# Transposes and products of two recurrent heads issued one step later, three results moved to other PSUM banks

## The chip, the cores and the metric

One Trainium2 chip, one core. The number is device microseconds (us) of one execution. Engines are named as in the profile: PE (TensorE matmul), PEld (TensorE weight load), DVE (VectorE), ACT (ScalarE), POOL (GpSimd), SP (SyncE, which issues nearly all DMAs). PSUM, where PE writes its results, has 8 banks of 2 KB per partition.

## The reference

One layer of a diffusion backbone with three recurrent branches, on 640 tokens (512 latent, 128 context) of width 1024, all in float32:

```
h   = RMSNorm(x) * (1 + scale1) + shift1
z   = h @ W_in                                   # cut into the columns of all branches
A   = HGRN2(q, f_fwd, f_bwd, i, g)               # 4 heads of 128, both directions
B   = RWKV7(...)                                 # 8 heads of 64, both directions
C   = mLSTM(q, k, v, o, gates)                   # 4 heads of 128, both directions
mix = (sig(gA)*(A @ P_A) + sig(gB)*(B @ P_B) + sig(gC)*(C @ P_C)) @ W_out
x   = x + gate1 * RMSNorm(mix)
x   = x + gate2 * RMSNorm(SwiGLU(RMSNorm(x) * (1 + scale2) + shift2))
```

HGRN and mLSTM are chunkwise. HGRN, for each chunk, makes the state S' = exp(b_end) * S + (k * exp(b_end - b))^T v and reads it with q * exp(b). mLSTM does C' = carry * C + (w * k)^T [v, 1], an inner product k^T q under a causal mask with exponential weights D, and num = D [v, 1] + w_inter * (q C). The outputs are the 640 tokens and the final states of the context.

## The kernel before, in words

Everything is kept transposed, features on partitions and the 640 tokens along the free axis. A projection by a 1024 x 128 block of weights is two halves of 320 tokens, each 8 blocks of k times 3 matmuls (`half_proj`): float32 is split into a high and a low part in a reduced format, and hi*hi, hi*lo and lo*hi are added up in one PSUM bank of the pool `pj`. The weights of a projection are two tiles of 512 columns, each split by ACT (`whi`, a cast, L344) and then DVE (`wlo`, the rest, L262), from a ring of 4 tiles (`WSB`), so two projections ahead at most.

The kernel goes through RWKV (up to about 605 us of the profile), then HGRN and mLSTM together (605 to 1003 us, the stage that is changed), then the merge, W_out and the feed-forward part. In the changed stage PSUM is cut into `pj` (4 banks: the halves of projections, and the accumulators `acc` and `col_` of the modulation rows), `ps` with tag "A" (2 banks: the results of mLSTM, among them `btr`, `ms`, `kv`, `kx`, `np_`, `nq`) and `ps2` with tag "H" (2 banks: HGRN's `btr`, `htr`, `hpr`, `hg_`, `hop`).

The order of the work is written as generators. `hgrn_head` and `mlstm_head` yield after each piece; `weave` takes two steps of HGRN for one of mLSTM; and `run_over` adds, after each step, `FILL2[head]` of a step of `fill`: the projections of the merge gates (evacuated by ACT at L572 into `gs`, which has two buffers and is written to DRAM) and the modulation's matmuls. What comes earlier in that order has precedence, but it is not the order on the engines. A list scheduler works through the program before it is compiled, with costs of its own for each instruction, takes on each engine the earliest instruction that it believes ready, and lets a tile wait for the release of its buffer or bank. The result is one fixed queue per engine, run in order: an instruction that waits holds up everything behind it on its engine, and the scheduler's costs are not the chip's.

A head of HGRN: project `hi` into `hT1`, transpose it to `v` by token (`by_token`, 5 transposes into 2 banks and 2 ACT copies), project `hq`, the two `hf`; exponentials and scans; for each direction transpose the keys `kh` (L1136), copy to `hkt` (ACT, L1138), multiply with `v` to `hpr` and add to the states (DVE, L268); then seven `level`s of intra-chunk products with POOL, DVE and ACT work; `hop`, output. A head of mLSTM: project `mv`, `mq`, `mk` and transpose two of them by token; `ms` = k^T q, masked on DVE to `mS`; for each direction the weights D, the state products `kv` and `kx`, then `np_` = D [v, 1] (copied by ACT to `nd`, L1394) and `nq` = q C (added by DVE, L268).

In the groups below, `hT` stands for HGRN's `hT1` and `hT2`, `nd` for the two `nd0`, `nd1`, and L277 is the line of all matmuls, L262 and L268 those of all DVE helper operations.

Of the kernel before, what the change touches and what calls it, by code (L numbers as in the profile page):

```python
# [8 lines left out]
F32 = mybir.dt.float32  # L9
# [33 lines left out]
RB2 = 2  # L43
HTB = 3
ORDER = "hoahoahoahoa" + "gga" * 12
FILL2 = (0.13, 0.14, 0.11, 0.16)
WSB = 4
RAWB = 3
YBB = 2
# [206 lines left out]
def build(tc, **A):  # L256
# [36 lines left out]
    with ExitStack() as top:  # L293
# [8 lines left out]
        pj_p = [pj_pool(6)]  # L302
# [742 lines left out]
        with ExitStack() as ms, ExitStack() as mr:  # L1045
# [33 lines left out]
            def hgrn_head(hd):  # L1079
                t1 = ht.tile([128, T], F32, name="hT1")  # L1080
                yield from mixproj(f"hi{hd}", h, to_sb(t1))
                v = hb.tile([128, 5, 128], F32, name="hv")
                by_token(v, t1, ps2, "H")
                yield
                q = hb.tile([128, T], F32, name="hq")
                yield from mixproj(f"hq{hd}", h, to_sb(q, 128.0 ** -0.5))
                yield
                b, kd, qe, SSs, zs, ls, khs, ebs = [], [], [], [], [], [], [], []
                D2 = range(2)
# [39 lines left out]
                for d in D2:  # L1129

                    S = hb.tile([128, 4, 128], F32, name=f"hS{d}")
                    sp.dma_start(S[:, 0 if d == 0 else 3], A["shg"][:, d * 4 + hd])
                    cs = (0, 1, 2, 4) if d == 0 else (3, 2, 1, 4)
                    tr = ps2.tile([128, 4, 128], F32, name="htr", tag="H")
                    for i, c in enumerate(cs):
                        pe.transpose(tr[:, i], khs[d][:, c * 128:(c + 1) * 128], ident)  # L1136
                    kt = ht.tile([128, 4, 128], F32, name="hkt", bufs=1)
                    act.copy(kt, tr)  # L1138
                    pr = ps2.tile([128, 4, 128], F32, name="hpr", tag="H")
                    for i, c in enumerate(cs):  # L1140
                        mm(pr[:, i], kt[:, i], v[:, c])
                    for i, c in enumerate(cs[:3]):
                        cn = c + 1 if d == 0 else c - 1
                        stt(S[:, cn], S[:, c], ebs[d][:, c:c + 1], pr[:, i], ALU.mult, ALU.add)
                    fs = ht.tile([128, 128], F32, name="hfs")
                    act.copy(fs, pr[:, 3])
                    sp.dma_start(A["ohg"][:, d * 4 + hd], fs)
                    SSs.append(S)
                    yield
# [192 lines left out]
            def mlstm_head(hd, mt):  # L1342
                k = mt.tile([128, T], F32, name="mk", bufs=1)
                yield from whole(mixproj(f"mv{hd}", h, to_sb(k)))
                by_token(v1, k, ps)
                q = mt.tile([128, T], F32, name="mq", bufs=1)
                k = mt.tile([128, T], F32, name="mk", bufs=1)
                yield from whole(mixproj(f"mq{hd}", h, to_sb(q)))
                yield from whole(mixproj(f"mk{hd}", h, to_sb(k, 128.0 ** -0.5)))
                kt = mt.tile([128, 5, 128], F32, name="mkt", bufs=1)  # L1350
                by_token(kt, k, ps)
                Sd = [mt.tile([128, 5, 128], F32, name=f"mS{d}", bufs=1) for d in range(2)]
                for c0, n in CP:
                    s_ = ps.tile([128, 4, 128], F32, name="ms", tag="A")
                    for i in range(n):
                        sl = slice((c0 + i) * 128, (c0 + i + 1) * 128)
                        mm(s_[:, i], k[:, sl], q[:, sl])
                    for d in range(2):
                        mul(Sd[d][:, c0:c0 + n], s_[:, :n], caus[:, d].unsqueeze(1).to_broadcast([128, n, 128]))
                nds, rds = [], []  # L1360
                for d in range(2):
                    ub = mt.tile([128, T], F32, name="ub", bufs=1)
                    sp.dma_start(ub, ud[d * 4 + hd:d * 4 + hd + 1].to_broadcast([128, T]))
                    D = mt.tile([128, 5, 128], F32, name="mD", bufs=1)
                    for c in range(5):
                        ts(D[:, c], c5(ub)[:, c], tcol("a", d, hd, c), 0.0, ALU.add, ALU.min)
                    act.activation(D, D, AF.Exp)
                    mul(D, D, Sd[d])
                    nd = mt.tile([128, 5, 129], F32, name=f"nd{d}", bufs=1)
                    Cs = mt.tile([128, 4, 129], F32, name="Cs", bufs=1)  # L1370
                    sp.dma_start(Cs[:, 0 if d == 0 else 3], A["scn"][:, d * 4 + hd])
                    vs = mt.tile([128, 5, 129], F32, name="vs", bufs=1)
                    pool.tensor_tensor(vs, v1, tcol("ws", d, hd).unsqueeze(2).to_broadcast([128, 5, 129]), ALU.mult)
                    kv = ps.tile([128, 3, 160], F32, name="kv", tag="A")
                    kx = ps.tile([128, 160], F32, name="kx", tag="A")
                    for i, c in enumerate((0, 1, 2) if d == 0 else (3, 2, 1)):
                        mm(kv[:, i, 0:129], kt[:, c], vs[:, c])
                        stt(Cs[:, c + 1 if d == 0 else c - 1], Cs[:, c], csb[:, d, hd, c:c + 1], kv[:, i, 0:129],
                            ALU.mult, ALU.add)
                    mm(kx[:, 0:129], kt[:, 4], vs[:, 4])  # L1380
                    C2 = mt.tile([128, 129], F32, name="Cn", bufs=1)
                    act.copy(C2, kx[:, 0:129])
                    sp.dma_start(A["ocn"][:, d * 4 + hd], C2)
                    yield
                    for c0, n in CP:
                        np_ = ps.tile([128, 3, 160], F32, name="np_", tag="A")
                        for i in range(n):
                            mm(np_[:, i, 0:129], D[:, c0 + i], v1[:, c0 + i])
                        nq = ps.tile([128, 3, 160], F32, name="nq", tag="A")
                        for i in range(n):  # L1390
                            c = c0 + i
                            if c < 4:
                                mm(nq[:, i, 0:129], q[:, c * 128:(c + 1) * 128], Cs[:, c])
                        act.copy(nd[:, c0:c0 + n], np_[:, :n, 0:129])  # L1394
                        for i in range(n):
                            c = c0 + i
                            if c < 4:
                                stt(nd[:, c], nq[:, i, 0:129], tcol("wi", d, hd, c), nd[:, c], ALU.mult, ALU.add)
                        yield
                    rd = mt.tile([128, 5], F32, name=f"rd{d}")  # L1400
                    den = nd[:, :, 128]
                    stt(rd, den, -1.0, den, ALU.mult, ALU.max)
                    tt(rd, rd, tcol("em", d, hd), ALU.max)
                    dve.reciprocal(rd, rd)
                    nds.append(nd)
                    rds.append(rd)
                hh = mt.tile([128, 5, 128], F32, name="mh", bufs=1)
                ssq = mt.tile([128, 5], F32, name="ssq")
                sq = mt.tile([128, 128], F32, name="msq")
                for c in range(5):  # L1410
                    ts(hh[:, c], nds[0][:, c, 0:128], rds[0][:, c:c + 1])
                    stt(hh[:, c], nds[1][:, c, 0:128], rds[1][:, c:c + 1], hh[:, c], ALU.mult, ALU.add)
                    act.activation(sq, hh[:, c], AF.Square, accum_out=ssq[:, c:c + 1])
                act.activation(ssq, ssq, AF.Sqrt, scale=1.0 / 128, bias=col(COL_EPS6))
                dve.reciprocal(ssq, ssq)
                for c in range(5):
                    ts(hh[:, c], hh[:, c], ssq[:, c:c + 1])
                og = mt.tile([128, T], F32, name="og", bufs=1)

                yield from need(24 + hd)  # L1420
                sp.dma_start(og, gates[24 + hd])
                yield
                ts(og, og, hmn[:, hd:hd + 1], hmn[:, hd:hd + 1])
                for c0, n in ((0, 4), (4, 1)):
                    tr = ps.tile([128, 4, 128], F32, name="mhtr", tag="A")
                    for i in range(n):
                        pe.transpose(tr[:, i], hh[:, c0 + i], ident)
                    mul(c5(yc[:, hd])[:, c0:c0 + n], tr[:, :n], c5(og)[:, c0:c0 + n])
# [403 lines left out]
```

## Time and profile before

| | |
|---|---|
| runs | 1619.7, 1621.25, 1624.62 us; median 1621.25 |
| the profiled execution | 1623.08 us, of which the span of its instructions is 1621.3 us |
| PE busy | 1540.6 us (95% of the span), PEld 1418.1 us |
| DVE busy | 1131.9 us (70%) |
| ACT busy | 782.8 us (48%) |
| POOL busy | 275.7 us (17%) |
| mean granted TensorE clock | 0.976 |

The chain that ended last is given to PE for 23% of the span by name and little else: PE is the engine that the rest is measured against. A row of the timeline is: start in us, duration in us, engine, line, operation, output and inputs, shape, how many instructions were merged in it, and in brackets how long the engine had been idle just before it and what ended that.

### The profile page before, as it was taken

What the parts mean: (1) busy time and instruction counts of PE and PEld (TensorE: products, weight loads), DVE (VectorE), ACT (ScalarE), POOL (GpSimd) and SP (SyncE); (2) the same over time, 40 slices, a digit from 0 to 9 for tenths busy, and PEclk for the clock granted to TensorE, in tenths of its full rate; (3) what the DMA queues carried; (4) which work ended last, traced back from release to release, by engine and by line L of the source; (5) the groups of instructions that cost most, each with busy time, mean ns of one, the idle gap of its engine ahead of it and who ended that gap; (6) DMA issues with size and microseconds to landing.
All of it is one profiled execution on the core that took longest, in us unless ns stands there. A gap on an engine that the chain in (4) does not pass through costs nothing. (4 is left out here: it accounts for less than half of the span.)

```text
span 1621.3 us, 34724 instructions
## 1 busy us (share of the span) xinstructions
PE 1540.6 (95%) x14194; PEld 1418.1 (87%) x14194; DVE 1131.9 (70%) x2355; ACT 782.8 (48%) x1546; POOL 275.7 (17%) x347
## 2 busy tenths in 40 slices
PE   6999999999999988899999999999999999999996
PEld 2988888888877778889798988999999999999996
DVE  6788788687777644786758578772887386586576
ACT  5364455454454334666476666223553343243244
POOL 2110110110110100211303031000123241341211
PEclk9999999999999969999999999999989999999998
DMA  9222222212122313232332332643512222222322
GB/s 361 71 75 88 74 71 80 95 50 88 66 73 95 113 49 103 70 99 78 94 100 85 100 101 95 201 145 108 155 37 86 95 79 76 82 88 68 99 94 97
DMA packets 63791, 157.35 MB, mean 97 GB/s; under 512 B 7432, under 2 KB 27912, under 8 KB 63504
## 3 DMA queue, kind: packets, MB, share of 16 engines
q1 hardware_dynamic: 63488, 155.13, 29.5%
q8 instruction: 111, 1.82, 0.5%
q14 instruction: 48, 0.39, 0.1%
q10 hardware_dynamic: 144, 0.00, 0.0%
HBM read 136.73 MB, written 18.37 MB: 96 GB/s over the span
## 5 line engine op out<-in xcount | busy, mean ns | idle before, releaser
L277 PE MATMUL pj<-h_hi,whi 128*128 128x320 f32 x1560 | 495.0, 320 | 5.4 <-ACT t L396 2.7
L277 PE MATMUL pj<-h_lo,whi 128*128 128x320 f32 x1560 | 494.4, 317 | 0.0
L277 PE MATMUL pj<-h_hi,wlo 128*128 128x320 f32 x1560 | 493.2, 317 | 0.0
L262 DVE TENSOR_TENSOR wlo<-raw,whi 128x512 fp32r<-128x512 f32 (+1 forms) x318 | 228.5, 726 | 130.7 <-ACT whi L344 106.2
L277 PEld LDWEIGHTS pj<-h_hi,whi 128*128 128x128 f32 x1560 | 296.3, 191 | 12.0 <-ACT t L396 3.7
L277 PEld LDWEIGHTS pj<-h_lo,whi 128*128 128x128 f32 x1560 | 296.7, 190 | 3.2
L277 PEld LDWEIGHTS pj<-h_hi,wlo 128*128 128x128 f32 x1560 | 296.9, 190 | 2.8
L344 ACT CAST whi<-raw 128x512 fp32r<-128x512 f32 (+1 forms) x264 | 156.8, 599 | 219.6 <-PE pj L277 209.4
L277 PE MATMUL pj<-a,whi 128*128 128x320 f32 x704 | 155.3, 309 | 0.0
L277 PEld LDWEIGHTS pj<-a,whi 128*128 128x128 f32 x704 | 117.7, 188 | 0.2
L277 PE MATMUL pj<-a,wlo 128*128 128x320 f32 x352 | 108.8, 309 | 0.0
L277 PE MATMUL pj<-t_hi,whi 128*128 128x320 f32 x288 | 89.1, 309 | 1.1 <-DVE u L262 1.1
L277 PE MATMUL pj<-t_hi,wlo 128*128 128x320 f32 x288 | 89.1, 309 | 0.1
L277 PE MATMUL pj<-t_lo,whi 128*128 128x320 f32 x288 | 89.0, 309 | 0.0
L262 DVE TENSOR_TENSOR wlo<-sm,whi 128x512 fp32r<-128x512 f32 x72 | 68.1, 946 | 11.4 <-ACT whi L1684 8.5
L1684 ACT CAST whi<-sm 128x512 fp32r<-128x512 f32 x72 | 44.4, 621 | 64.4 <-PE pj L277 50.2
L1678 POOL TENSOR_TENSOR sm<-raw 128x512 f32<-128x512 f32 x36 | 49.0, 1360 | 110.3 <-DMA raw<-wff 72.5
L277 PEld LDWEIGHTS pj<-a,wlo 128*128 128x128 f32 x352 | 66.1, 188 | 0.0
L277 PE MATMUL pj<-hl,whi 128*128 128x320 f32 x256 | 56.5, 310 | 0.6 <-ACT hl L1462 0.6
L1684 ACT CAST whi<-raw 128x512 fp32r<-128x512 f32 x54 | 33.5, 620 | 45.6 <-PE pj L277 37.7
L277 PEld LDWEIGHTS pj<-t_hi,whi 128*128 128x128 f32 x288 | 54.1, 188 | 1.3 <-DVE u L262 1.3
L277 PE MATMUL acc<-raw,sc 128*32 128x256 f32 (+1 forms) x320 | 40.7, 437 | 14.8 <-DMA raw<-wada 14.8
(659 smaller groups left out, 2988.0 us busy)
## 6 DMA issues: line engine op xcount, KB each, us to landing
raw<-wmix SPq DMA_DIRECT2D x76, 512.0 KB, 3.5
raw<-wada SPq DMA_DIRECT2D x48, 512.0 KB, 5.6
raw<-wff SPq DMA_DIRECT2D x44, 512.0 KB, 3.7
gates<-gs SPq DMA_DIRECT2D x64, 160.0 KB, 1.8
raw<-wff SPq DMA_DIRECT2D x24, 384.0 KB, 3.2
gs<-gates SPq DMA_DIRECT2D x24, 320.0 KB, 3.1
raw<-wbr SPq DMA_DIRECT2D x12, 512.0 KB, 4.3
raw<-wout SPq DMA_DIRECT2D x8, 512.0 KB, 5.0
```

What stands on the lines that cost most here:

```text
L262: dve.tensor_tensor(out, a, b, op)
L277: newest[0] = pe.matmul(out, lhsT=lhsT, rhs=rhs, start=start, stop=stop, skip_group_check=more).ins
L344: act.copy(hi[:, :w], raw[:, o:o + w])
L1678: pool.tensor_tensor(o, x, y, op)
L1684: act.copy(hi, x)
```

## The change

Three pieces of work are placed elsewhere in the generators, three tiles come from another PSUM pool, and the rates at which `fill` is mixed in are lowered by 0.01.

- HGRN: `by_token` of `v` comes after the projection `hq` and no longer before it (the number of yields stays).
- HGRN: a yield stands between the copy `hkt` and the products `hpr` (two more per head).
- mLSTM: a yield stands between the transposes of k and the products `ms` (one more per head). The woven stage has 171 steps, where it had 159.
- mLSTM: `ms`, `kx` and `nq` take a bank of `pj` (4 banks) and no longer one of `ps` "A" (2 banks).

```
--- before.py
+++ after.py
@@ -43,7 +43,7 @@
 RB2 = 2
 HTB = 3
 ORDER = "hoahoahoahoa" + "gga" * 12
-FILL2 = (0.13, 0.14, 0.11, 0.16)
+FILL2 = (0.12, 0.13, 0.1, 0.15)
 WSB = 4
 RAWB = 3
 YBB = 2
@@ -1079,11 +1079,11 @@
             def hgrn_head(hd):
                 t1 = ht.tile([128, T], F32, name="hT1")
                 yield from mixproj(f"hi{hd}", h, to_sb(t1))
+                yield
                 v = hb.tile([128, 5, 128], F32, name="hv")
-                by_token(v, t1, ps2, "H")
-                yield
                 q = hb.tile([128, T], F32, name="hq")
                 yield from mixproj(f"hq{hd}", h, to_sb(q, 128.0 ** -0.5))
+                by_token(v, t1, ps2, "H")
                 yield
                 b, kd, qe, SSs, zs, ls, khs, ebs = [], [], [], [], [], [], [], []
                 D2 = range(2)
@@ -1136,6 +1136,7 @@
                         pe.transpose(tr[:, i], khs[d][:, c * 128:(c + 1) * 128], ident)
                     kt = ht.tile([128, 4, 128], F32, name="hkt", bufs=1)
                     act.copy(kt, tr)
+                    yield
                     pr = ps2.tile([128, 4, 128], F32, name="hpr", tag="H")
                     for i, c in enumerate(cs):
                         mm(pr[:, i], kt[:, i], v[:, c])
@@ -1349,9 +1350,10 @@
                 yield from whole(mixproj(f"mk{hd}", h, to_sb(k, 128.0 ** -0.5)))
                 kt = mt.tile([128, 5, 128], F32, name="mkt", bufs=1)
                 by_token(kt, k, ps)
+                yield
                 Sd = [mt.tile([128, 5, 128], F32, name=f"mS{d}", bufs=1) for d in range(2)]
                 for c0, n in CP:
-                    s_ = ps.tile([128, 4, 128], F32, name="ms", tag="A")
+                    s_ = pj_p[0].tile([128, 4, 128], F32, name="ms", tag="pj")
                     for i in range(n):
                         sl = slice((c0 + i) * 128, (c0 + i + 1) * 128)
                         mm(s_[:, i], k[:, sl], q[:, sl])
@@ -1372,7 +1374,7 @@
                     vs = mt.tile([128, 5, 129], F32, name="vs", bufs=1)
                     pool.tensor_tensor(vs, v1, tcol("ws", d, hd).unsqueeze(2).to_broadcast([128, 5, 129]), ALU.mult)
                     kv = ps.tile([128, 3, 160], F32, name="kv", tag="A")
-                    kx = ps.tile([128, 160], F32, name="kx", tag="A")
+                    kx = pj_p[0].tile([128, 160], F32, name="kx", tag="pj")
                     for i, c in enumerate((0, 1, 2) if d == 0 else (3, 2, 1)):
                         mm(kv[:, i, 0:129], kt[:, c], vs[:, c])
                         stt(Cs[:, c + 1 if d == 0 else c - 1], Cs[:, c], csb[:, d, hd, c:c + 1], kv[:, i, 0:129],
@@ -1386,7 +1388,7 @@
                         np_ = ps.tile([128, 3, 160], F32, name="np_", tag="A")
                         for i in range(n):
                             mm(np_[:, i, 0:129], D[:, c0 + i], v1[:, c0 + i])
-                        nq = ps.tile([128, 3, 160], F32, name="nq", tag="A")
+                        nq = pj_p[0].tile([128, 3, 160], F32, name="nq", tag="pj")
                         for i in range(n):
                             c = c0 + i
                             if c < 4:
```

## Rows read from the trace of the kernel before

**Rows 1.** Windows (us; busy of PE, PEld, DVE, ACT, POOL; clock, DMA share, GB/s), changed stage
```profile
605.00:700.00 95.00, 84.65 (x650) 80.74 (x648) 59.68 (x103) 53.16 (x95) 14.96 (x16) 0.93 0.31 98
700.00:792.00 92.00, 87.70 (x884) 82.97 (x884) 65.09 (x147) 59.09 (x119) 17.60 (x20) 1.00 0.28 91
792.00:884.00 92.00, 89.23 (x893) 84.06 (x892) 67.17 (x151) 59.25 (x120) 19.00 (x20) 1.00 0.30 91
884.00:977.00 93.00, 88.80 (x891) 83.90 (x890) 65.93 (x149) 59.28 (x119) 17.60 (x20) 1.00 0.30 90
977.00:1003.00 26.00, 24.34 (x361) 21.50 (x359) 23.28 (x70) 15.52 (x40) 2.80 (x4) 1.00 0.21 65
```

**Rows 2.** Waits of PE, 605 to 1003 us (waiter, releaser: total us, times, longest)
```profile
PE nq L277 <- ACT nd L1394: 5.8, 6, 1.5
PE hpr L277 <- ACT hkt L1138: 5.4, 3, 5.0
PE btr L557 <- ACT hT L396: 4.2, 1, 4.2
PE ms L277 <- ACT mkt L558: 3.5, 3, 1.5
```

**Rows 3.** Timeline of PE, first head, around the two long stalls
```profile
612.36 0.69 PE L557 MATMUL btr<-cst,hT 128*128 128x128 f32 x2 [4.16 <-ACT hT L396]
612.70 0.61 PE L277 MATMUL pj<-h_hi,whi 128*128 128x320 f32 x1
...
617.68 0.31 PE L277 MATMUL pj<-h_lo,whi 128*128 128x320 f32 x1
617.83 0.30 PE L277 MATMUL pj<-h_hi,wlo 128*128 128x320 f32 x1
...
669.45 0.31 PE L277 MATMUL pj<-h_hi,wlo 128*128 128x320 f32 x1
674.73 2.07 PE L277 MATMUL hpr<-hv,hkt 128*128 128x128 f32 x8 [4.96 <-ACT hkt L1138]
...
679.00 0.33 PE L277 MATMUL pj<-h_hi,whi 128*128 128x320 f32 x1
```

**Rows 4.** Windows of 10 us around these two stalls
```profile
610.00:620.00 10.00, 7.64 (x37) 7.60 (x38) 9.69 (x20) 7.28 (x13) 0.00 (x0) 0.66 0.06 15
670.00:680.00 10.00, 5.28 (x24) 5.28 (x25) 7.53 (x15) 4.21 (x9) 0.81 (x1) 0.66 0.27 89
```

**Rows 5.** Timeline of ACT, first head
```profile
609.96 1.28 ACT L1308 ACT_TABLE_LOAD   x1 [3.01 <-DVE mrow L1280]
...
672.33 1.54 ACT L1194 ACTIVATE hT<-hT 128x640 f32<-128x640 f32 x2 [1.82 <-DVE hT L262]
```

**Rows 6.** Timeline of DVE, first head, two weight splits
```profile
619.33 1.29 DVE L262 TENSOR_TENSOR wlo<-raw,whi 128x512 fp32r<-128x512 f32 x2
...
673.02 0.68 DVE L262 TENSOR_TENSOR wlo<-raw,whi 128x512 fp32r<-128x512 f32 x1
```

**Rows 7.** Timeline of ACT, second head
```profile
776.58 0.44 ACT L572 ACTIVATE gs<-pj 128x320 f32<-128x320 f32 x1 [2.61 <-DMA gates<-gs]
...
788.50 0.48 ACT L1394 COPY nd<-np__10419 128x387 f32<-128x387 f32 x1
```

**Rows 8.** Timeline of PE, second head
```profile
777.44 1.16 PE L277 MATMUL ms<-mq,mk 128*128 128x128 f32 x8 [1.47 <-ACT mkt L558]
778.83 1.16 PE L277 MATMUL hpr<-hv,hkt 128*128 128x128 f32 x8 [0.23 <-ACT hkt L1138]
...
789.03 0.94 PE L277 MATMUL nq<-Cs,mq 128*128 128x129 f32 x6 [1.26 <-ACT nd L1394]
...
791.66 0.49 PE L277 MATMUL nq<-Cs,mq 128*128 128x129 f32 x2 [0.66 <-ACT nd L1394]
```

**Rows 9.** Timeline of DVE, second head
```profile
788.86 0.35 DVE L268 SCALAR_TENSOR_TENSOR Cs<-Cs,csb,kv 128x129 f32<-128x129 f32 x1
...
796.28 0.34 DVE L268 SCALAR_TENSOR_TENSOR nd<-nq,TM,nd 128x129 f32<-128x129 f32 x1
```

More of the change, by code (lines that the diff above doesn't have):

```diff
@@ L45 @@
 ORDER = "hoahoahoahoa" + "gga" * 12
-FILL2 = (0.13, 0.14, 0.11, 0.16)
+FILL2 = (0.12, 0.13, 0.1, 0.15)
 WSB = 4
@@ L1081, in hgrn_head @@
                 yield from mixproj(f"hi{hd}", h, to_sb(t1))
+                yield
                 v = hb.tile([128, 5, 128], F32, name="hv")
-                by_token(v, t1, ps2, "H")
-                yield
                 q = hb.tile([128, T], F32, name="hq")
                 yield from mixproj(f"hq{hd}", h, to_sb(q, 128.0 ** -0.5))
+                by_token(v, t1, ps2, "H")
                 yield
@@ L1138, in hgrn_head @@
                     act.copy(kt, tr)
+                    yield
                     pr = ps2.tile([128, 4, 128], F32, name="hpr", tag="H")
@@ L1351, in mlstm_head @@
                 by_token(kt, k, ps)
+                yield
                 Sd = [mt.tile([128, 5, 128], F32, name=f"mS{d}", bufs=1) for d in range(2)]
                 for c0, n in CP:
-                    s_ = ps.tile([128, 4, 128], F32, name="ms", tag="A")
+                    s_ = pj_p[0].tile([128, 4, 128], F32, name="ms", tag="pj")
                     for i in range(n):
@@ L1374, in mlstm_head @@
                     kv = ps.tile([128, 3, 160], F32, name="kv", tag="A")
-                    kx = ps.tile([128, 160], F32, name="kx", tag="A")
+                    kx = pj_p[0].tile([128, 160], F32, name="kx", tag="pj")
                     for i, c in enumerate((0, 1, 2) if d == 0 else (3, 2, 1)):
@@ L1388, in mlstm_head @@
                             mm(np_[:, i, 0:129], D[:, c0 + i], v1[:, c0 + i])
-                        nq = ps.tile([128, 3, 160], F32, name="nq", tag="A")
+                        nq = pj_p[0].tile([128, 3, 160], F32, name="nq", tag="pj")
                         for i in range(n):
```

## The prediction

> **What bounds the kernel now.** I read the busy times first (PE 95% of the span), then the windows of the changed stage, then PE's waits in it, and for each wait the timeline of PE and of the engine that ended it. The windows [rows 1] show that PE is idle for 10.35, 4.30, 2.77, 4.20 and 1.66 us of the five stretches, 23.3 us in all; everywhere else PE works through projections. So a stall of PE that goes is worth its length, unless PE meets another wait straight after it, and nothing else in the stage is worth anything. Four waits carry 18.9 of these 23.3 us: `nq` 5.8, `hpr` 5.4, `btr` 4.2, `ms` 3.5 [rows 2]. These are exactly the operations that the change touches, so what can be gained is bounded, and the question is what PE meets next.
>
> Two stalls cost more than their length. After 4.16 and 4.96 us of standing [rows 3] the granted clock of the two windows is 0.66 on average [rows 4], which mixes the two levels, 1.2 and 2.4 GHz. PE comes back at the lower one: from 612.36 to 617.68 and from 674.73 to 679.00, where the timeline shows starts 0.27 us apart and not 0.15, so half of 5.32 and half of 4.27 us is lost, 2.7 and 2.1 us. In the later heads, where no stall is over 1.5 us [rows 2], the clock stays at 1.00 [rows 1].
>
> **The change part by part.** The sum is made against the profiled execution, 1623.08 us (1621.3 of span and 1.8 around it); it lies 1.83 us above the median of the runs, so I take the sum off the median.
>
> No instruction is added or removed: the same transposes, products, copies and DMAs are issued, 12 steps of the woven order hold nothing new, and the lower rates of `fill` over 171 steps instead of 159 put about as many of its steps beside each head (0.13 x 39 = 5.1 and 0.12 x 42 = 5.0 in the first). Counting the yields by hand, the fill projections come to within one or two steps of where they were; one shift matters: the fill projection of the first head that came right after the first `hpr` now comes before it. The cost of these at 0 rests on PE having projections to run in the meantime; without that cover, a step is worth at most the 1.66 us that PE is idle at the stage's end [rows 1].
>
> *Moving `by_token` of v (term A).* In the first head PE stands 4.16 us because the transposes wait for ACT's copy of `hi` [rows 3], and ACT stood 3.01 us for a scan of the mLSTM gates on DVE before a table load [rows 5]. The matmuls of `hq` follow the transposes at once [rows 3], so their weights were there. In the new order PE runs `hq` from 608.2: 48 matmuls, 0.15 us from one start to the next at the full clock (617.68 to 617.83 [rows 3]), are 7.2 us, to 615.4, and the five transposes end by about 616. But the next projection needs a `wlo` that DVE makes only at 619.33 [rows 6], behind the chain of gate operations that keeps it busy 9.69 of 10 us [rows 4], and those are not moved. PE then waits until about 620 instead, some 4 us, and the clock most likely falls again. The bounds are 0 and 4.16 + 2.7 = 6.8 us; I take 0.5. In the later heads there was no such wait (one in all [rows 2]), so nothing is gained there.
>
> *The yield before `hpr` (term B).* The long one of three waits is 4.96 us at 674.73 [rows 3]. The copy `hkt` came late because ACT, in its own order, stood for DVE before the exponentials of a level (1.82 us at 672.33) [rows 5]. With the fill projection ahead of `hpr`, PE goes on with it: the row at 669.45 is the sixth of 12 matmuls on its first weight tile, ended by 669.76; it does 6 more (0.9 us) and then lacks the second tile, whose `wlo` DVE makes from 673.02 to 673.70 [rows 6]. So it stands about 3.0 us, not 4.96: 1.9 us gained. Whether a stall of 3 us still costs clock no row shows, since the nearest are 1.5 us (no) and 4.16 us (yes). I add 0.6 of the 2.1 us: 2.5. Bounds 0 and 7.1. `hpr`, the state sums behind it on DVE and the DMA of the final state come a step later; DVE has other work then, and the levels do not read the states.
>
> The Trainium skill (TensorE: Matmul & The Clock Gate, Part 1) says that the low rate is the default and that activity releases it; by that alone, a stall that still counts as idle keeps the whole loss and B is 1.9, one that does not gives B 4.0. Its Part 4 says that transposes do not count as matmul activity in the same way, which speaks against term A, where ten transposes of the gates would come right after the new stall: the slow stretch with transposes in it was 5.32 us and the one without 4.27 [rows 3], so A would lose half of 1.05, about 0.5 us, and be 0. Neither changes the sum by more than the bounds above.
>
> *The yield before `ms`, and its banks (term C).* `ms` reads only the projections of q and k; it waited for the copies `mkt`, because with two banks in "A" its bank was that of the transposes. In the second head this is 1.47 us at 777.44 [rows 8]. With `pj` it need not wait for that. But ACT itself stood 2.61 us until 776.58 for the DMA that empties `gs` [rows 7], and the second `hpr` waits for a copy behind the same ACT instruction: it came 0.23 us after `ms` [rows 8]. If the queue puts that `hpr` ahead of `ms`, as the new yields make likely, PE stands at the same place for `hkt`, and `ms` no longer covers it. Per head the result lies between -1.4 us (1.16 us of `ms` uncovered and the 0.23) and +1.5; over the three waits 3.5 us is the upper end and -3 the lower. I take 1.0, nearer the middle.
>
> *`nq` and `kx` in `pj` (term D).* `nq` waited for the bank that ACT's copy of `np_` gives back: 1.26 us at 789.03 and 0.66 at 791.66 in the second head [rows 8], with the copy at 788.50 [rows 7]. Its data, the states `Cs` of the first chunks, were there. With its own bank it starts at once, about 787.8, and takes 0.8 us. Then the second `np_` needs a bank of "A", free at 788.98 (the copy) or 789.21 (the last sum out of `kv`) [rows 7, 9], so 0.4 to 0.6 us of waiting comes back. Gained 0.7 to 0.8 of the 1.26 and all of the 0.66, say 1.4 of 1.92. In that ratio the 5.8 us give 4.2; since the queue around it will be another, I take 3.5, bounds 0 and 5.8. `kx` had no wait of its own and counts 0.
>
> *What the moved tiles take from projections (term E).* A bank with `nq` is held until DVE has added it: from 791.66 to 796.62, 5.0 us [rows 8, 9]. The `pj` pool has four banks, a half projection takes 24 x 0.15 = 3.6 us of one and then waits for its evacuation, and `acc` and `gs` hold banks in the same stretch. Bounds: 0 (a bank is always free) and -14 (worked out under the rivals). I take -1.0, nearest to 0, because three of four banks must be out at once.
>
> Sum: 0.5 + 2.5 + 1.0 + 3.5 - 1.0 = 6.5 us off. From 1623.08 that is 1616.6 for a like execution, and from the median 1614.75: I say 1615.
>
> **The rivals.**
> *Given back.* Each stall comes back as a wait one step on: A as a wait for `wlo`, B too with the clock lost again, C as a wait for `hkt`. For it: DVE is all but full where A ends [rows 4], and ACT's late copies have causes that the change leaves alone [rows 5, 7]. Against it: the `nq` waits have no second cause near. A 0, B 0.5, C 0, D 2.0, E -0.5: 2 us, 1619.25.
> *Starved projections.* PE finds no free `pj` bank when a half projection begins, because `ms` and `nq` wait for DVE. Each hold of 5.0 us leaves 1.4 us beyond the 3.6 us of the half that PE can still run. There are five such holds in a head (`ms`, and `nq` twice in each direction), 20 in all; if half of them strike, 14 us is lost against the 7.5 us gained, 6.5 us slower: 1627.75. It decides from the point where three of the four banks are waiting for DVE or ACT. For it: DVE takes 5 us to come to `nq` [rows 8, 9]. Against it: the four banks were never what PE waited for [rows 2].
> *All of it.* The stalls go and PE finds work everywhere: 0.5 + 7.1 + 3.5 + 0.5 (the short `hpr` waits) + 5.8 = 17.4 us, 1604. It needs DVE to make its low parts earlier than now, for which no row speaks.
>
> **How the numbers follow.** Forecast 0.45, given back 0.25, starved 0.20, all of it 0.10. What can be told from no change here is 0.3%, 4.9 us: below 1616.4 or above 1626.1. The forecast's own spread is 1610 to 1619, two thirds of it below 1616.4: 0.30; with all of it 0.10 and a fifth of the second case 0.05, faster is 0.45. Slower is most of the starved case and a trace of the second, 0.17; the rest, 0.38, is no change. The range for 8 in 10 goes from 1607, which leaves out most of the last case, to 1626, which leaves out most of the starved one.
>
> **What would show it.** Right: the waits of PE lose the rows of `nq` on `nd` and `ms` on `mkt`, PE's idle time between 605 us and the stage's end falls from 23 to about 17 us, and the stall at 612 is found some 8 us later, ended by DVE's `wlo`. B is wrong if `hpr` still waits some 5 us for `hkt`, or if the clock stays at 1.00 around 675. C is wrong if `hpr` waits longer for `hkt` in heads two to four than the 0.23 us of now. E shows as waits of a first `pj` matmul for DVE's `nd` or `mS`. The forecast as a whole is wrong if the difference comes from before 605 us or after the stage, where nothing is edited, or if PE's busy time in the stage rises at full clock.

## The result, and the profile after

The changed kernel takes 1676.22 us (median of 4 runs, 1668.16 to 1678.36), the kernel before 1622.16 us (4 runs): a ratio of 1.0335, 95% interval 1.0313 to 1.0358. I had said 1615, with 1607 to 1626 as the range: the sign and the size are both wrong. The profiled execution of after is its fastest, 1668.16 us with a span of 1666.3 us, 45.0 us over the span of before.

First the engines' busy times over the span, from the page of after:

```profile
PE 1545.7 (93%) x14194; PEld 1428.6 (86%) x14194; DVE 1136.4 (68%) x2355; ACT 789.1 (47%) x1548; POOL 276.0 (17%) x347
```

The same 14194 matmuls; PE was busy 1540.6 us before. Then the windows of the changed stage, which now ends about 1048 us and not 1003 (columns as in rows 1):

```profile
605.00:700.00 95.00, 81.04 (x708) 78.18 (x707) 62.00 (x110) 53.77 (x97) 17.16 (x18) 0.94 0.31 99
700.00:803.00 103.00, 90.34 (x849) 86.82 (x849) 66.28 (x146) 59.71 (x119) 18.12 (x20) 0.93 0.26 79
803.00:900.00 97.00, 86.39 (x766) 84.23 (x766) 59.51 (x132) 55.40 (x108) 11.99 (x14) 0.90 0.23 76
900.00:1004.00 104.00, 89.58 (x836) 85.25 (x837) 64.58 (x142) 58.67 (x115) 16.37 (x18) 0.91 0.25 80
1004.00:1048.00 44.00, 34.24 (x467) 30.89 (x468) 33.46 (x95) 23.21 (x55) 9.25 (x11) 0.77 0.24 74
```

The stage is 443 us long and was 398. PE idles 61.4 of them (23.3 in [rows 1]): 38.1 us more. It is busy 381.6 us (374.7 in [rows 1]) though it holds slightly fewer matmuls (3624 in the trace of this stretch, 3671 before: a little of `fill` now comes after it), because the granted clock is 0.77 to 0.94 where it was 1.00 after the first head: 6.9 us more. The two make the 45.0 us; the stretches before and after the stage are as long as they were.

PE's waits in that stage, to be put beside [rows 2]:

```profile
PE hpr L277 <- ACT hkt L1138: 13.2, 4, 3.4
PE mtr L1314 <- ACT PK L1307: 5.8, 1, 5.8
PE kv L277 <- DVE Cs L268: 3.7, 4, 1.1
PE hg__10475 L277 <- DVE hT L262: 2.8, 1, 2.8
...
PE hg__12871 L277 <- DVE rd L268: 2.1, 1, 2.1
...
PE nq L277 <- DVE Cs L268: 1.7, 4, 0.5
```

The waits of `nq` for `nd` and of `ms` for `mkt` are gone, as the change means, and `btr`'s too. In their place stand longer ones: `hpr` in every head, and the levels (`hg_`) of every head, 1.8 to 2.8 us at each of three or four levels, 31 us in all where the levels of before waited 3. No row shows a projection that waits for a bank. PE's timeline of the second head, from the second state product to the last levels, shows why the levels' waits are there:

```profile
787.05 1.16 PE L277 MATMUL hpr<-hv,hkt 128*128 128x128 f32 x8 [3.41 <-ACT hkt L1138]
788.14 1.24 PE L277 MATMUL hg__10297<-hT,hT 128*64 128x64 f32 x20
789.31 2.08 PE L277 MATMUL ms<-mq,mk 128*128 128x128 f32 x8
...
800.21 0.56 PE L277 MATMUL hg__10442<-hT,hT 128*32 128x32 f32 x40 [0.28 <-DVE hT L262]
803.60 0.76 PE L277 MATMUL hg__10475<-hT,hT 128*32 128x32 f32 x40 [2.83 <-DVE hT L262]
806.53 0.76 PE L277 MATMUL hg__10515<-hT,hT 128*32 128x32 f32 x40 [2.17 <-DVE hT L262]
809.11 0.77 PE L277 MATMUL hg__10548<-hT,hT 128*32 128x32 f32 x40 [1.81 <-DVE rd L268]
810.96 0.80 PE L277 MATMUL kv<-vs,mkt 128*128 128x129 f32 x2 [1.08 <-DVE Cs L268]
```

From 781.24 to 820.79 there is not one projection matmul between these rows. In the kernel before, projections filled exactly these gaps; the same levels there, with the first and the last projection matmul of a gap:

```profile
793.33 0.56 PE L277 MATMUL hg__10442<-hT,hT 128*32 128x32 f32 x40
793.82 0.42 PE L277 MATMUL pj<-h_hi,wlo 128*128 128x320 f32 x1
...
795.83 0.31 PE L277 MATMUL pj<-h_hi,whi 128*128 128x320 f32 x1
796.41 0.56 PE L277 MATMUL hg__10475<-hT,hT 128*32 128x32 f32 x40 [0.28 <-DVE hT L262]
...
802.12 0.56 PE L277 MATMUL hg__10548<-hT,hT 128*32 128x32 f32 x40
```

From `hg__10442` to `hg__10548` the levels take 8.8 us before and 8.9 after: they did not get slower, only what ran beside them is gone. Two windows over levels of the second head, first before (a longer one), then after:

```profile
790.00:808.00 18.00, 17.06 (x297) 15.43 (x296) 17.83 (x46) 8.73 (x15) 3.02 (x5) 1.00 0.19 55
```

```profile
799.50:811.00 11.50, 3.32 (x165) 2.67 (x164) 11.41 (x32) 3.81 (x8) 1.96 (x2) 0.61 0.42 125
```

DVE is full in both, 17.83 of 18 and 11.41 of 11.5 us, and the levels wait for it. PE was busy 17.06 of the 18 us beside it and now is 3.32 of the 11.5. The compiled queue of PE says the same. Counted between a head's first `ms` and its `hop`, it holds 78, 83, 78 and 83 projection matmuls in the four heads before, and 0, 0, 0, 0 after. In the second head the tiles are these, in the order of the queue (the numbers rise with the order of the program):

```
before: ... col_  pj_10719 ... hg__10397  nq_10423 ... hg__10442  pj_10719 pj_10745 ... pj_10816 ... nq_10700  hop ...
after:  ... nq_10423 ... hg__10442 hg__10475 hg__10515 hg__10548 ... np__10696  nq_10700  hop  nq_10700  pj_10719 ...
```

`pj_10719` to `pj_10816` are four half projections: the two of the next head's `hi` and two of `fill`'s merge gates, which ACT copies to `hT1` and to `gs`. Later in the program than `nq_10700`, the second direction's `nq`, they ran before it; now the first waits until `nq_10700`, which is of its pool since the change, has its bank. In both queues the first matmuls of all the pool's tiles in this stage stand in the order of their numbers, without an exception.

### The profile page after: what moved, and what is told of

It reads as the page before. It is cut to its first block, busy times and chain, and to the rows that moved or that the text cites. A ratio compares the mean times of both kernels' runs of the same rounds, so it can differ in the third digit from the quotient of the medians.

```text
span 1666.3 us, 34731 instructions
## 1 busy us (share of the span) xinstructions
PE 1545.7 (93%) x14194; PEld 1428.6 (86%) x14194; DVE 1136.4 (68%) x2355; ACT 789.1 (47%) x1548; POOL 276.0 (17%) x347
## 5 line engine op out<-in xcount | busy, mean ns | idle before, releaser
L277 PEld LDWEIGHTS pj<-t_hi,wlo 128*128 128x128 f32 x288 | 54.1, 188 | 0.7 <-DVE wlo L262 0.7
```

What stands on the lines that cost most here:

```text
L277: newest[0] = pe.matmul(out, lhsT=lhsT, rhs=rhs, start=start, stop=stop, skip_group_check=more).ins
```

## The experiments

**Theory (order of the pool):** a pool's banks are given out in the order of the program, so a tile that is ready late, `nq` of the second direction, holds back every projection behind it in the program, and nothing runs beside the levels. **Rivals:** the moved pieces and yields (steps); too few free banks because `ms`, `nq` and `kx` hold them for DVE (count, the prediction's starved case). Each kernel was timed beside the kernel before, whose medians were 1619.9 to 1621.3 us.

### Which part of the change

`steps_only` keeps all moves, yields and rates and takes the three tiles back; `banks_only` is the reverse:

```
 steps_only:  after, with  s_, kx, nq = ps.tile(..., tag="A")
 banks_only:  before, with s_, kx, nq = pj_p[0].tile(..., tag="pj")
```

> The changed kernel with ms, kx and nq back in the two banks of A; the moved pieces, the three yields and the fill rates stay. Theory (order of the pool): the banks of pj are given out in the order of the program, so nq of the second direction, which stands in the program before the projections of the next head, keeps these from starting early, and PE has nothing to run between the levels. Then the moved pieces are harmless: 1612 to 1626 us, and PE idles 20 to 26 us in the stage. Rival (steps): the state products one step later lengthen HGRN's chain, and their waits for hkt (13.2 us in the changed kernel) are the start of the loss: 1645 us or more. Rival (count of banks): as the theory, since no tile is moved.

> The kernel before with only ms, kx and nq moved to pj; no yield, no moved piece, the old fill rates. Order of the pool: nearly the whole loss, 1660 to 1680 us, with no projection matmul on PE between ms and hop of a head. Count of banks: the same time, but with first matmuls of a projection waiting for DVE's nd or mS. Steps: 1630 us or less.

`steps_only` 1627.82 us (ratio 1.0035, 1.0021 to 1.0048), `banks_only` 1686.19 us (1.0388, 1.0369 to 1.0408). The steps cost some 6 us and not 25; the banks cost more alone than with the steps, and a little more than the 1680 us that the theory allowed. In `banks_only` too the queue holds no projection matmul between `ms` and `hop`, and no row shows a projection that waits for `nd` or `mS`, as the count of banks would have it. `steps_only` came out a little over what the theory allowed it: the moves are not harmless, see below.

### Which tile

```
 nq_only:  after, with s_ and kx back in ps "A"
 nq_back:  after, with nq back in ps "A"
```

> The changed kernel with only nq in pj; ms and kx back in A. Order of the pool: the second direction's nq alone stands before the next projections and needs the last states, so the loss stays, 1655 to 1680 us. Count of banks: ms takes two banks and kx one, so without them about half of the loss is left: 1635 to 1650 us. Steps: 1645 us or more here too.

> The changed kernel with nq back in A; ms and kx stay in pj. Order of the pool: ms and kx need only projections, transposes and one POOL product and come early, so the projections of the next head are held back little: 1614 to 1634 us. Count of banks: two banks of ms and one of kx are still taken, so half of the loss is left: 1640 to 1655 us. Steps: 1645 us or more.

`nq_only` 1688.58 us (1.0409, 1.0385 to 1.0433), a little above what was expected; `nq_back` 1631.55 us (1.0052, 1.0036 to 1.0069). It is `nq`.

### Which direction of it, and order or number

```
 nq_d0, nq_d1:  before, with nq = (pj_p[0] if d == 0 else ps)...   or   d == 1
 pj3:           before, with PJ2 = 3
 nq_own:        pj3, with px = tile_pool(bufs=1, space=PSUM);  nq = px.tile(...)
```

> The kernel before with nq in pj for the second direction only. Order of the pool: this nq is the last pj tile before the next head's projections and needs the last of the head's states, so nearly the whole loss of 54 to 67 us is here: 1665 to 1690 us. Count of banks: half of the nq tiles, so at most half of the loss: 1640 to 1655 us.

> The kernel before with nq in pj for the first direction only. Order of the pool: it gets its bank while the first levels still run and the projections can start behind it: 1616 to 1635 us. Count of banks: as many tiles as the second direction's, so the same time as with those, 1640 to 1655 us.

> The kernel before with nq in a PSUM pool of its own of one bank, pj cut from four to three banks. Order of the pool: projections have a bank less, but nothing of mLSTM stands in their pool, so they run ahead again: 1618 to 1640 us, about as the kernel with only pj cut to three. Count of banks: projections have three banks here as they had with an nq that holds one, so the loss stays: 1660 us or more.

> The kernel before with pj cut from four banks to three, one bank unused, nothing else: what a lost bank alone costs. Order of the pool: 1618 to 1635 us. Count of banks: 1650 us or more.

`nq_d1` 1681.79 us (1.0368, 1.0343 to 1.0392): half the tiles, the whole loss. `nq_d0` 1630.86 us (1.0047, 1.0031 to 1.0063). The queue of PE holds 0 projection matmuls beside the levels in each head of `nq_d1`, 68 or 69 in those of `nq_d0`. `nq_own` 1632.90 us (1.0071, 1.0051 to 1.0090), with three banks for projections and `nq` in no one's way: the 60 us are not a matter of number. `pj3` 1642.85 us (1.0131, 1.0112 to 1.0150) is slower than expected, so a bank is worth 21.6 us to the projections: its queue holds 48, 67, 48 and 83 of their matmuls between `ms` and `hop`, and none beside the last three levels of heads one and three. With the same three banks, `nq` out of "A" gains 10 us (1642.85 to 1632.90).

The last pair changes the program order of the same tiles by the weave alone:

```
 hr18_before:  before, with HRATE = 1.8        hr18_d1:  nq_d1, with HRATE = 1.8
```

> nq_d1 (nq of the second direction in pj, nothing else) with the weave at 1.8 steps of HGRN for one of mLSTM and no longer 2: mLSTM's products then stand earlier in the program order against HGRN's levels. Order of the pool: the loss of 60 us against the kernel before depends on that order, and with nq earlier some projections stand behind it beside the levels (25 of them in the first head, 151 in the last, where nq_d1 had none), so this lies at most 25 us above the same weave without the moved tile. Run time holding of banks (count): the moved tile costs 50 to 60 us in this weave too.

> The kernel before with the weave at 1.8: the control for the other run, what the weave costs by itself. No theory fixes it: it shifts the streams against each other; 1625 to 1660 us.

`hr18_before` 1658.08 us (1.0230, 1.0197 to 1.0263), `hr18_d1` 1676.03 us (1.0333, 1.0300 to 1.0366). With the tile in `pj`, 18 us more, where the usual weave has 60 us more (1681.79 against 1621.27). With `nq` earlier in the program, against the levels, the same tile costs a third. The queues agree: between `ms` and `hop` they hold 85, 85, 101 and 151 projection matmuls in the four heads of `hr18_before` and 25, 56, 101 and 151 in those of `hr18_d1`, so 89 are lost, and none in the last two heads; `nq_d1` lost all 322. By these numbers, as an estimate, each costs about 0.2 us in both weaves (18 over 89, 60 over 322). The order of the program decides, not the time that a bank is held.

### What the moved pieces cost by themselves

```
 bytoken:    before, by_token(v, ...) behind hq        hpr_yield: before, yield after act.copy(kt, tr)
 ms_yield:   before, yield after by_token(kt, k, ps)   ms_pj:     before, ms in pj
```

> The kernel before with only by_token of v moved behind the projection hq. Term A of the prediction: the 4.16 us stall is found some 8 us later, as a wait for the gates' chain on DVE (in the changed kernel it is 5.8 us, before mtr): 1619 to 1623 us, no difference from before. Rival (A is the loss of the moved pieces): about the 5.6 us that the moved pieces cost together, 1626 us or more.

> The kernel before with only the yield before the state products. Theory (steps): the yield puts hpr behind a projection in one place and ahead of other work in another, and hpr then waits some 3.4 us for hkt in every head (13.8 us with all three moves): this alone costs 3 to 8 us, 1624 to 1630 us. Rival (term B as predicted): 2.5 us faster, 1618 to 1620 us.

> The kernel before with only the yield before ms. It makes mLSTM's stream one step longer in each head, so that mLSTM falls behind HGRN from head to head, and fewer projections stand between ms and hop in the last two heads. Theory (the projections beside the levels are what counts): slower, 1626 to 1645 us, with PE idle between the levels of heads three and four. Rival (term C as predicted): within 2 us of before.

> The kernel before with only ms in pj. Order of the pool: ms needs nothing but the projections of q and k, so it holds no projection back; its 3.5 us of waits for mkt go: 1616 to 1621 us. Rival (given back): the next hpr waits for hkt instead, 1620 to 1624 us.

`bytoken` 1625.66 us (1.0033, 1.0021 to 1.0046), `hpr_yield` 1645.35 us (1.0166, 1.0148 to 1.0184), `ms_yield` 1630.86 us (1.0071, 1.0057 to 1.0085), `ms_pj` 1624.53 us (1.0026, 1.0014 to 1.0038). None gains. `ms_yield` lies in the theory's range; `bytoken` lies above the range for term A and beside its rival's 1626; `ms_pj` lies at the end of its rival's range (given back), not in the theory's; and `hpr_yield` costs three times what I allowed it, not by the waits that I named (`hpr` waits only 4.4 us for `hkt` in it). In PE's waits of the stage, of `bytoken` and then of `ms_pj`, each stall that was taken away is back one step on, to be compared with [rows 2]:

```profile
PE mtr L1313 <- ACT PK L1306: 5.8, 1, 5.8
PE nq L277 <- ACT nd L1394: 5.8, 6, 1.5
```

```profile
PE hpr L277 <- ACT hkt L1138: 9.7, 3, 5.0
PE nq L277 <- ACT nd L1394: 4.6, 4, 1.4
```

Without its `btr` wait of 4.2 us, PE stands 5.8 us before the gates' transposes. Without its `ms` waits of 3.5 us, `hpr` stands 9.7 us and not 5.4. What `hpr_yield` loses is at the end of the stage; its windows, then those of before:

```profile
900.00:985.00 85.00, 81.97 (x685) 78.07 (x671) 49.76 (x114) 51.85 (x103) 9.27 (x12) 1.00 0.30 91
985.00:1030.00 45.00, 28.22 (x436) 24.37 (x434) 35.09 (x88) 25.20 (x58) 7.61 (x10) 0.77 0.23 74
```

```profile
900.00:985.00 85.00, 80.89 (x764) 76.66 (x763) 58.00 (x122) 56.50 (x115) 16.36 (x18) 1.00 0.31 93
985.00:1030.00 45.00, 43.03 (x370) 40.60 (x369) 38.73 (x99) 24.33 (x55) 1.15 (x2) 0.96 0.51 165
```

Two steps more in each of four heads of HGRN, and mLSTM as it was, leave HGRN's last levels to the end (its last `hop` starts at 1018.0 us and not at 995.7, while mLSTM's last `mhtr` is at 1008.4 and was at 1009.8), where few projections are left to run beside them (the queue has none beside the last five levels of the last head): PE has 28.22 us of work in 45 and the clock averages 0.77. With the yield in mLSTM as well, the streams are 28 to 14 steps a head, as they were 26 to 13, and `steps_only` loses only 6 us. So the three single costs don't add up, and in `steps_only` only part of the 6 us is placed: `hpr` waits 13.8 us for `hkt` in it and `mtr` 5.8, while `nq`'s, `ms`'s and `btr`'s waits are short or gone. `bytoken`, with the same wait before `mtr`, loses 5.8 us alone; whether the two yields together cost next to nothing was not run.

No version here beats the kernel before.

## Why the prediction was wrong, point by point

- *The frame held.* The loss is where the edits are, PE's idle time and its clock account for all of it, and DVE, ACT and the rest have the same work. PE's idle time in the stage, which was to fall from 23 to about 17 us, rose to 61.
- *Term E is the step that failed.* I put the moved tiles at -1.0 us "nearest to 0, because three of four banks must be out at once", and priced only banks in use. That one tile which is not ready keeps all later ones of its pool from getting a bank, however many are free, is the mechanism. It costs 44.7 of the 54 us by the medians: that is what `nq_back` gets back (1676.22 to 1631.55). The starved rival named the pool, but its price, 14 us, was a third of this, its point of decision was wrong, and the waits that it asked for (`pj` on `nd` or `mS`) never appear, since the loss lies in the order of the queue. My argument against it, that the four banks were never what PE waited for, was no evidence: `pj3` loses 21.6 us without such a wait. The trace of before could have shown it: PE is only 0.94 us idle in 18 us in which DVE makes the levels, and the projections that fill them belong to the next head and to the steps of `fill` behind this one, so they run ahead of the program. What the cover costs when it goes was asked for each moved step; for the pool it was not.
- *Term A:* the wait came back at the time that I gave (the transposes of the gates start at 619.43 us, 7 us later than the stall of [rows 3]) but for ACT's `PK` and not for a `wlo`, and longer, 5.80 us. By the medians `bytoken` loses 5.8 us instead of gaining 0.5; the new wait is only 1.6 us longer than the old, and where the rest goes is not shown.
- *Term B:* in the first head the wait of 4.96 us before the first direction's `hpr` is gone, but the second direction's now waits 3.19 us, and heads two to four, where `hpr` waited 0.23 us at most, have 3.3 to 3.4 us each. The clock stayed at 1.00 from 670 to 680 us, which I had named as a sign against this term. The yield alone costs 25 us (`hpr_yield`): that it lengthens one of two streams by eight steps I had put at 1.66 us at most, and this is the larger part (PE idles 16.78 of the last window's 45 us above, where it idled 1.97).
- *Term C:* the mechanism of its lower end was right (and three heads at -1.4 us are -4.2, not -3). In the second head `hpr` stands 3.41 us because ACT, ahead of `hkt`, waits for the DMA that empties `gs`, as [rows 7] had it. ACT's rows of the changed kernel there:

```profile
786.09 0.44 ACT L572 ACTIVATE gs<-pj 128x320 f32<-128x320 f32 x1 [3.28 <-DMA gates<-gs]
786.42 0.58 ACT L1138 COPY hkt<-htr 128x512 f32<-128x512 f32 x1
```

  `ms` no longer covers that time, as four of its five products now stand behind `hpr`, and `ms_pj` is 4.6 us slower, where I had 1.0 faster and 3 slower as the worst.
- *Term D* was right in kind and too small: with the order out of the way, `nq` out of "A" is worth 10 us (`pj3` to `nq_own`), not 3.5, and more than its upper bound, 5.8.
- *The clock.* Whether a stall of 3 us costs the higher level, no row showed. It does here: after the 3.41 us the window from 788 to 792 averages 0.57, a mix of the two levels. In the levels, with 2.83, 2.17 and 1.81 us of idling in a row, the clock falls again, and it is at 0.50, which is 1.2 GHz, from 803 to 819 us, though PE is busy 6.43 of the last 7. It is back at 1.00 in the products of `hop`, before the first projection at 820.79. Windows of the changed kernel:

```profile
787.00:788.00 1.00, 0.95 (x8) 0.95 (x8) 0.00 (x0) 1.00 (x4) 0.00 (x0) 1.00 0.53 178
788.00:792.00 4.00, 4.00 (x36) 3.76 (x35) 3.17 (x9) 1.48 (x4) 1.40 (x2) 0.57 0.52 150
792.00:800.00 8.00, 6.86 (x127) 5.05 (x125) 6.60 (x16) 4.53 (x11) 4.76 (x5) 1.00 0.19 35
800.00:803.00 3.00, 0.56 (x40) 0.45 (x40) 3.00 (x7) 1.11 (x3) 1.96 (x2) 0.82 0.87 265
803.00:806.00 3.00, 0.76 (x40) 0.62 (x40) 3.00 (x8) 1.37 (x2) 0.00 (x0) 0.50 0.39 124
806.00:812.00 6.00, 2.54 (x99) 2.06 (x103) 5.91 (x20) 1.80 (x3) 0.00 (x0) 0.50 0.13 50
812.00:819.00 7.00, 6.43 (x66) 6.07 (x58) 3.79 (x13) 0.90 (x2) 1.14 (x2) 0.50 0.11 36
819.00:822.00 3.00, 3.00 (x26) 3.00 (x26) 0.86 (x3) 1.93 (x10) 0.00 (x0) 1.00 0.11 27
```

The Trainium skill (Perfetto Trace Analysis, Identifying Performance Opportunities) reads the same gap, repeated over a stretch, as a sign that SBUF or PSUM may be short. The gaps of the levels repeat in each head here, and the pool is PSUM's; but `nq_own`, which has one bank less for the projections, is 49 us faster than `nq_d1`. `pj3` agrees with that rule: a bank less costs 21.6 us there. For the moved tile the runs narrow it: what was short was a place in line and not a bank.

Not settled: why `banks_only` loses 10 us more than the change as a whole, and how the 6 us of `steps_only` divide.

## What to carry to other kernels

Before a tile goes to another pool, list what stands behind it in that pool in the order of the program, and ask when it gets ready: where buffers are given out in that order, as here, a late tile stops work that used to run ahead, however many are free. The work that filled the gaps of DVE's stage was worth more here (44.7 us) than all four waits that the profile listed (18.9); find out which work that is, and price the case that it comes later. And a yield put into one of two woven streams shifts their balance: the yields cost 25 and 11 us in one stream alone, while the kernel with all of them lost 6.

## What the runs showed that I had not expected

One bank of four is worth 21.6 us to projections that are never seen to wait for one (`pj3`, 1642.85 against 1621.27). And the cause of a wait can be missing from the list of waits: in the changed kernel no row names `pj`, while the levels' waits for DVE grew from 3 to 31 us, because the projections that covered them stand too late in PE's queue.
